# The down-projection's columns as seven block products, its steps spread over the next part's up-projection

## The chip, the core and the metric

The kernel runs on one core of one Trainium2 chip. The metric is device microseconds of one execution of the program. A profile is taken of one execution; its span runs from the first to the last instruction that the profile shows, and the execution's own time is a little longer. All lengths below are in microseconds (us) unless marked ns.

## What is computed

One layer of a streaming encoder, on 256 tokens of width 2048 in fp32. An attention half (two groups of eight heads with a combined input projection and an output projection) comes first and isn't touched in what it computes. The second half is the feed-forward network (FFN), cut here to what matters:

```python
def conv_ffn(h, w_up, conv_w, conv_b, w_down):
    u = h @ w_up                                  # 256 x 2048 @ 2048 x 11264
    u = causal_depthwise_conv(u, conv_w, width=3) + conv_b
    gate, val = jnp.split(u, 2, axis=-1)          # 256 x 5632 each
    return (jax.nn.silu(gate) * val) @ w_down     # 5632 x 2048

x = x + hybrid_mixer(rms_norm(x), ...)            # attention, output projection
x = x + conv_ffn(rms_norm(x), ...)
```

## The kernel before

Matmuls run in fp32r. To keep fp32 accuracy every operand is split into a rounded part `hi` and a remainder `lo`, and a product is three matmuls: hi x hi, hi x lo and lo x hi. Activations are split once and kept; weights are split as they stream in. `weights` (lines 202 to 215) does that for a tile of 128 x 2048 (1 MiB): a DMA on SyncE's queue into `w_raw` (three buffers), a cast on ScalarE into `w_hi` (line 210, two buffers) and a subtraction on VectorE into `w_lo` (line 211, two buffers). The three instructions are put 200 instructions ahead of their place in the program's order of priority (`AHEAD`). The framework orders each engine's instructions by priority and readiness when the program is built; on the chip every engine runs its own list in order.

The kernel has these stages:

- Up to about 413 us: input projection, both attention groups and the output projection. `token_major` (lines 220 to 240) is the projection with tokens on the partitions: the activation tile is the stationary operand, 512 weight columns are the moving one, and per k tile and token tile it issues three matmuls (lines 235 to 237) into an accumulator of two PSUM banks (`psa`, two of them). `next_rows` (line 535) transposes the normalized x into `hT` for the FFN while the output projection ends; `sums_of_squares` (line 163) reads each quarter of x with the scratch tile `junk`. The attention has its own pools `at`, `tmp` (SBUF) and `pss` (PSUM), which close at line 563; the weight buffers (`wpool`) are one pool for the whole kernel.
- The FFN (lines 563 to 633), in three parts of 16, 16 and 12 column tiles of 128 (`FFN_PARTS`). For each part first all of its up-projection, then its down-projection.
- Up-projection: `up_pair` (line 603) makes two column tiles over all 256 tokens. `feature_major` (lines 242 to 260) loads and splits the weights in two halves of eight k tiles; per k and column tile there is one matmul of 512 moving columns (hi of the weights by hi and lo of the activations, line 250) and one of 256 (lo by hi, line 255). Accumulators rotate over three places, two in `psa` and one in `psf`. `convolved` (lines 582 to 601) empties the accumulator (`summed`, lines 262 to 267: a copy on ScalarE and an addition on VectorE), multiplies by the token factors `R` (line 588) into one of four `up` buffers, and makes the convolution (ScalarE line 592, VectorE line 597, two taps per tile). A gate pair and a value pair give the gated activations, split into `g2` (lines 620 to 624).
- Down-projection: for each part and each 512 of the 2048 output columns, `token_major` over the part's k tiles, and an addition of the two token tiles into x in SBUF (line 630). After the last part the results are written out, 512 columns at a time (line 633).

`step` (line 192) is called after each weight tile's matmuls, and lets generators in `waiting` (attention heads, transposes) issue their next piece between two weight tiles.

Of the kernel before, what the change touches and what calls it, by code (L numbers as in the profile page):

```python
# [24 lines left out]
NFT = DFF // P  # L25
# [11 lines left out]

AHEAD = 200
WINDOW = 2
FFN_PARTS = [(0, 16), (16, 32), (32, 44)]  # L40


@with_exitstack
def hybrid_layer(
# [19 lines left out]
    nc = tc.nc  # L64
    act, dve = nc.scalar, nc.vector
# [7 lines left out]
    wpool = ctx.enter_context(tc.tile_pool(name="wpool", bufs=3))  # L73
# [12 lines left out]
    crow = const.tile([NC2, 4, P], F32, name="crow")  # L86
# [21 lines left out]
    def load_parameters(masks):  # L108
        r0 = KT
        for src, n in (  # L110
            (ffn_norm, KT), (out_norm_fox, NH), (out_norm_sb, NH), (q_norm, 1), (k_norm, 1)
        ):
            nc.sync.dma_start(prow[r0 : r0 + n, :], src[0].rearrange("(n p) -> n p", p=P))
            r0 += n
        nc.sync.dma_start(cs[:, P:], cst[:, P:C_MF])
        nc.sync.dma_start(masks, cst[:, C_MF:])
        nc.sync.dma_start(bf, b_forget.to_broadcast([P, NH]))
        nc.sync.dma_start(crow[:, :3, :], conv_w[0].rearrange("w (n p) -> n w p", p=P))
        nc.sync.dma_start(crow[:, 3, :], conv_b[0].rearrange("(n p) -> n p", p=P))

    def rsqrt(out_, ss, scale, n):
        a = small.tile([P, n], F32, name="rs_a", tag=f"rs_a{n}")
# [55 lines left out]
            dve.tensor_scalar(dg[t], ident, rstd[:, t : t + 1], None, op0=ALU.mult)  # L178
        return rstd, dg

    def in_every_partition(dg, n):
        R = const.tile([P, S], F32, name=f"R{n}")
        pr = psb.tile([P, S], F32, name="pr", tag="t")
        for t in range(NT):
            nc.tensor.matmul(pr[:, t * P : (t + 1) * P], ones, dg[t], start=t == 0, stop=t == NT - 1)
        dve.tensor_copy(R, pr)
        return R


    waiting = deque()  # L190

    def step():
        for g in list(waiting)[:WINDOW]:
            if next(g, g) is g:
                waiting.remove(g)
# [3 lines left out]
            step()  # L199


    def weights(src, a, b):
        raw = wpool.tile([P, 2048], F32, name="w_raw", tag="w_raw")
        hi = wpool.tile([P, 2048], F32R, name="w_hi", tag="w_hi", bufs=2)
        lo = wpool.tile([P, 2048], F32R, name="w_lo", tag="w_lo", bufs=2)
        n = a * b
        r3 = raw[:, :n].rearrange("p (a b) -> p a b", a=a)
        with tc.high_priority(offset=AHEAD):
            nc.sync.dma_start(r3, src)
            act.copy(hi[:, :n], raw[:, :n])  # L210
            dve.tensor_tensor(lo[:, :n], raw[:, :n], f32(hi[:, :n]), op=ALU.subtract)  # L211
        return (
            hi[:, :n].rearrange("p (a b) -> p a b", a=a),
            lo[:, :n].rearrange("p (a b) -> p a b", a=a),
        )

    def rows_of(w, k0, n, c0, cols):
        return w[k0 * P : (k0 + n) * P, c0 : c0 + cols].rearrange("(k p) c -> p k c", p=P)
# [23 lines left out]
    def feature_major(w, c0, pool, tag):  # L242

        acc = pool.tile([P, 2, 512], F32, name="pu", tag=tag)
        for kh in range(2):
            hi, lo = weights(rows_of(w, 8 * kh, 8, c0, 2 * P), 8, 2 * P)
            for i in range(8):
                k = 8 * kh + i
                for j in range(2):
                    nc.tensor.matmul(  # L250
                        acc[:, j, :], hi[:, i, j * P : (j + 1) * P],
                        hT[:, k].rearrange("p a b -> p (a b)"), start=k == 0, stop=False,
                    )
                for j in range(2):
                    nc.tensor.matmul(  # L255
                        acc[:, j, S:], lo[:, i, j * P : (j + 1) * P], hT[:, k, 0, :],
                        start=False, stop=k == KT - 1,
                    )
            step()
        return acc  # L260

    def summed(pool, acc, tag, **kw):

        t2 = pool.tile([P, 2, S], F32, name="t2", tag=tag, **kw)
        act.copy(t2, acc[:, :, S:])
        dve.tensor_tensor(t2, acc[:, :, :S], t2, op=ALU.add)
        return t2

    with ExitStack() as actx:
        at = actx.enter_context(tc.tile_pool(name="at", bufs=1))  # L270
        pss = actx.enter_context(tc.tile_pool(name="pss", bufs=2, space=bass.MemoryType.PSUM))
        tmp = actx.enter_context(tc.tile_pool(name="tmp", bufs=2))
# [77 lines left out]
        rstd1, dg1 = token_factors(ss1, 1)  # L350
# [19 lines left out]
        for j in range(3):  # L370
            acc = project(2 * WF + 344 * j, 344)
# [97 lines left out]


        B0 = 3 * WF + NH
        R1 = in_every_partition(dg1, 1)
        R1q = const.tile([P, S], F32, name="R1q")
        dve.tensor_scalar(R1q, R1, QSCALE, None, op0=ALU.mult)

        def sb_heads(c0, scale, name):
# [87 lines left out]
    ccol = const.tile([P, 4, NC2], F32, name="ccol")  # L564
    R = None

    def convolution_parameters():
# [6 lines left out]
    ff = ctx.enter_context(tc.tile_pool(name="ff", bufs=2))  # L574
    psf = ctx.enter_context(tc.tile_pool(name="psf", bufs=1, space=bass.MemoryType.PSUM))
    nu = 4
    up = [ff.tile([P, 2, 2 + S], F32, name=f"up{i}") for i in range(nu)]
    for u in up:
        dve.memset(u[:, :, 0:2], 0.0)
    n_up = 0  # L580

    def convolved(ps, f0):

        nonlocal n_up
        u = up[n_up % nu]
        n_up += 1
        t2 = summed(ff, ps, "t2")
        dve.tensor_tensor(u[:, :, 2:], t2, R.unsqueeze(1).to_broadcast([P, 2, S]), op=ALU.mult)  # L588
        a = ff.tile([P, 2, S], F32, name="cv", tag="cv", bufs=4)
        for j in range(2):  # L590
            f = f0 + j
            act.activation(  # L592
                a[:, j, :], u[:, j, 2:], AF.Identity,
                scale=ccol[:, 2, f : f + 1], bias=ccol[:, 3, f : f + 1],
            )
            for w in range(2):
                dve.scalar_tensor_tensor(  # L597
                    a[:, j, :], u[:, j, w : w + S], ccol[:, w, f : f + 1], a[:, j, :],
                    op0=ALU.mult, op1=ALU.add,
                )  # L600
        return a

    def up_pair(f0):

        nonlocal R, n_pair
        pool, tag = (psf, "pu") if n_pair % 3 == 2 else (psa, "acc")
        n_pair += 1
        acc = feature_major(wu, f0 * P, pool, tag)
        if R is None:
            R = in_every_partition(dg2, 2)  # L610
            convolution_parameters()
        return convolved(acc, f0)

    gT = {}
    n_pair = 0
    for n_part, (f_lo, f_hi) in enumerate(FFN_PARTS):
        for f in range(f_lo, f_hi, 2):
            gate = up_pair(f)
            val = up_pair(NFT + f)
            act.activation(gate, gate, AF.Silu)  # L620
            dve.tensor_tensor(gate, gate, val, op=ALU.mult)
            g2 = ff.tile([P, 2, 2, S], F32R, name="g2", tag="g2", bufs=12)
            act.copy(g2[:, 0], gate)  # L623
            dve.tensor_tensor(g2[:, 1], gate, f32(g2[:, 0]), op=ALU.subtract)
            for j in range(2):
                gT[f + j] = g2[:, :, j, :]
        for c in range(4):
            acc = token_major(lambda k: gT[f_lo + k], wd, f_lo, f_hi - f_lo, 512 * c, 512)
            xs = x2[:, :, c * 512 : (c + 1) * 512]
            dve.tensor_tensor(xs, acc, xs, op=ALU.add)  # L630
            if n_part == len(FFN_PARTS) - 1:
                for t in range(NT):
                    nc.sync.dma_start(of[t * P : (t + 1) * P, c * 512 : (c + 1) * 512], xs[:, t, :])


def _constants():
# [54 lines left out]
```

## Time and profile before

| | us |
|---|---|
| median of 3 runs (1151.68 to 1153.18) | 1152.29 |
| the profiled execution | 1153.37 |
| its span | 1151.6 |
| TensorE matmuls busy (share of the span) | 1137.1 (99%) |
| VectorE busy | 716.4 (62%) |
| ScalarE busy | 551.9 (48%) |

Lines of the profile name the source line, the engine, the operation and the tiles (`out<-in`). PE is TensorE's matmuls, PEld its weight loads, DVE VectorE, ACT ScalarE, SPq the queue of SyncE that issues the DMAs. Matmul records overlap, since the array is pipelined: what one costs in a row of many is the distance from start to start. In the timeline an "x2" merges neighbours of one kind. A releaser, after "<-", is what the profile shows as the last thing that an instruction waited for.

### The profile page before, as it was taken

How to read it: one execution, taken by the hardware profiler on the slowest of the kernel's cores; microseconds unless marked ns; L12 is line 12 of the kernel's file. 1: busy time of each engine (PE TensorE's matmuls, PEld its weight loads, DVE VectorE, ACT ScalarE, POOL GpSimd, SP SyncE). 2: the span in 40 equal slices, each digit the busy share in tenths (PEclk: the TensorE clock that was granted, in tenths of full speed). 3: DMA queues.
4: the chain of work that ended last, by engine and by line, in shares of the span. 5: the costliest groups of instructions: out<-in, count | busy, mean ns of one | idle time of the engine just before them, and what ended most of it. 6: DMA issues, size and time to landing. Idle time of an engine off the chain costs nothing.

```text
span 1151.6 us, 14371 instructions
## 1 busy us (share of the span) xinstructions
PE 1137.1 (99%) x6002; PEld 976.7 (85%) x6002; DVE 716.4 (62%) x798; ACT 551.9 (48%) x620; POOL 0.2 (0%) x4
## 2 busy tenths in 40 slices
PE   7999999999999999999999999999999999999998
PEld 5998888888888888888888888888888888888886
DVE  4646756646565667677774546767775455767753
ACT  4644454455564555555554334555554334555531
POOL 0000000000000000000000000000000000000000
PEclk9999999999999999999999999999999999999999
DMA  6766555564445545555556655555556655555562
GB/s 227 213 210 204 170 173 161 168 182 148 147 149 170 185 154 193 195 194 185 183 183 198 203 183 186 194 196 192 184 183 188 204 193 183 187 195 193 189 221 74
DMA packets 162540, 211.39 MB, mean 184 GB/s; under 512 B 3737, under 2 KB 117547, under 8 KB 162475
## 3 DMA queue, kind: packets, MB, share of 16 engines
q1 hardware_dynamic: 162474, 210.47, 56.7%
q8 instruction: 47, 0.77, 0.3%
q14 instruction: 19, 0.15, 0.0%
HBM read 208.36 MB, written 2.10 MB: 183 GB/s over the span
## 4 chain that ended last, share of the span: by engine, by line
PE 96%; DVE 1%; ACT 1%; DMA 1%; issue 1%; SPq 0%; ACTq 0%; DVEq 0%
PE pu L250 34%; PE pu L255 17%; PE acc L236 14%; PE acc L237 14%; PE acc L235 14%; ACT w_hi L210 1%; DVE w_lo L211 1%; PE ps_x L152 1%; DMA w_raw<-in_w_in_dram 0%; DMA masks<-in_cst_dram 0%; PE ps_z L492 0%; PE ps_h L284 0%; PE ps_s L425 0%; PE ps_o L452 0%; PE ps_o L518 0%
## 5 line engine op out<-in xcount | busy, mean ns | idle before, releaser
L211 DVE TENSOR_TENSOR w_lo<-w_raw,w_hi 128x2048 fp32r<-128x2048 f32 (+2 forms) x204 | 450.8, 2210 | 360.2 <-ACT w_hi L210 360.2
L210 ACT CAST w_hi<-w_raw 128x2048 fp32r<-128x2048 f32 (+2 forms) x204 | 375.9, 1843 | 512.4 <-issue 260.5
L250 PE MATMUL pu<-hT,w_hi 128*128 128x512 f32 x1664 | 523.5, 396 | 0.0
L255 PEld LDWEIGHTS pu<-hT,w_lo 128*128 128x128 f32 x1664 | 312.4, 188 | 73.9 <-DVE w_lo L211 0.4
L255 PE MATMUL pu<-hT,w_lo 128*128 128x256 f32 x1664 | 327.6, 278 | 0.0
L250 PEld LDWEIGHTS pu<-hT,w_hi 128*128 128x128 f32 x1664 | 253.8, 189 | 0.3
L236 PE MATMUL acc<-w_lo,g 128*128 128x512 f32 x352 | 137.1, 389 | 0.8 <-DVE w_lo L211 0.8
L235 PE MATMUL acc<-w_hi,g 128*128 128x512 f32 x352 | 137.1, 389 | 0.0
L237 PE MATMUL acc<-w_hi,g 128*128 128x512 f32 x352 | 136.9, 389 | 0.0
L235 PE MATMUL acc<-w_hi,hT 128*128 128x512 f32 (+1 forms) x320 | 120.2, 376 | 0.0
L236 PE MATMUL acc<-w_lo,hT 128*128 128x512 f32 (+1 forms) x320 | 119.2, 373 | 0.5 <-DVE w_lo L211 0.3
L237 PE MATMUL acc<-w_hi,hT 128*128 128x512 f32 (+1 forms) x320 | 119.0, 372 | 0.0
L236 PEld LDWEIGHTS acc<-w_lo,g 128*128 128x128 f32 x352 | 66.1, 188 | 14.8 <-DVE w_lo L211 1.3
L235 PEld LDWEIGHTS acc<-w_hi,g 128*128 128x128 f32 x352 | 66.1, 188 | 13.8 <-ACT g L623 0.3
L237 PEld LDWEIGHTS acc<-w_hi,g 128*128 128x128 f32 x352 | 66.1, 188 | 13.8
L597 DVE SCALAR_TENSOR_TENSOR cv<-up,ccol,cv 128x256 f32<-128x256 f32 x176 | 74.2, 480 | 2.2 <-ACT cv L592 2.0
L236 PEld LDWEIGHTS acc<-w_lo,hT 128*128 128x128 f32 x320 | 60.5, 189 | 9.6 <-DVE w_lo L211 1.5
L237 PEld LDWEIGHTS acc<-w_hi,hT 128*128 128x128 f32 x320 | 60.6, 189 | 8.8
L235 PEld LDWEIGHTS acc<-w_hi,hT 128*128 128x128 f32 x320 | 60.6, 189 | 8.1
L592 ACT ACTIVATE cv<-up,ccol 128x256 f32<-128x256 f32 x88 | 48.2, 591 | 8.0 <-DVE up L588 8.0
L235 PE MATMUL acc<-w_hi,oT 128*128 128x512 f32 x96 | 38.1, 397 | 0.0
L237 PE MATMUL acc<-w_hi,oT 128*128 128x512 f32 x96 | 37.5, 390 | 0.0
(146 smaller groups left out, 602.4 us busy)
## 6 DMA issues: line engine op xcount, KB each, us to landing
w_raw<-in_w_up_dram SPq DMA_DIRECT2D x88, 1024.0 KB, 5.1
w_raw<-in_w_down_dram SPq DMA_DIRECT2D x44, 1024.0 KB, 5.1
w_raw<-in_w_in_dram SPq DMA_DIRECT2D x36, 1024.0 KB, 5.3
w_raw<-in_w_out_dram SPq DMA_DIRECT2D x16, 1024.0 KB, 5.1
w_raw<-in_w_in_dram SPq DMA_DIRECT2D x12, 688.0 KB, 4.3
w_raw<-in_w_in_dram SPq DMA_DIRECT2D x8, 512.0 KB, 5.3
out_dram<-x SPq DMA_DIRECT2D x8, 256.0 KB, 3.6
x<-in_x_dram SPq DMA_DIRECT2D x3, 512.0 KB, 6.2
```

The lines of the kernel that those rows point to most:

```text
L152: nc.tensor.transpose(ps[:, j, t * P : (t + 1) * P], xt[t][:, (k + j) * P : (k + j + 1) * P], ident)
L210: act.copy(hi[:, :n], raw[:, :n])
L211: dve.tensor_tensor(lo[:, :n], raw[:, :n], f32(hi[:, :n]), op=ALU.subtract)
L235: nc.tensor.matmul(o, lhi, hi[:, i, :], start=first, stop=False)
L236: nc.tensor.matmul(o, lhi, lo[:, i, :], start=False, stop=False)
L237: nc.tensor.matmul(o, llo, hi[:, i, :], start=False, stop=last)
L250: nc.tensor.matmul(acc[:, j, :], hi[:, i, j * P : (j + 1) * P], hT[:, k].rearrange("p a b -> p (a b)"), start=k == 0, stop=False,)
L255: nc.tensor.matmul(acc[:, j, S:], lo[:, i, j * P : (j + 1) * P], hT[:, k, 0, :], start=False, stop=k == KT - 1,)
L592: act.activation(a[:, j, :], u[:, j, 2:], AF.Identity, scale=ccol[:, 2, f : f + 1], bias=ccol[:, 3, f : f + 1],)
L597: dve.scalar_tensor_tensor(a[:, j, :], u[:, j, w : w + S], ccol[:, w, f : f + 1], a[:, j, :], op0=ALU.mult, op1=ALU.add,)
```

## The change

The FFN is cut into six parts, five of eight column tiles and one of four. A part's down-projection is no longer done after its up-projection: it is made a generator, put into `behind`, and issued in steps between the weight tiles of the next part's up-projection. Each weight tile of the up-projection adds `pace` (14, in the last part 22) to a counter, and each 16 of it issue one step, so 14 steps lie among a part's 16 weight tiles, and 11 among the last part's 8. The last part's own down-projection follows at the end as before.

For the first four parts all of the columns, and for the fifth half of them, are computed in blocks: the part's eight k tiles are two row blocks of the weights, 1024 output columns are two column blocks of 512, and the two token tiles are the activation's two. These 2 x 2 x 2 block products are made as seven, on sums and differences of blocks. `combinations` makes four differences or sums of activation blocks for each two pairs, on VectorE, and splits them. `down_in_seven` loads weight blocks, adds them on VectorE, splits each of the seven, multiplies it (12 matmuls, `product`), and adds the bank into x (`add`); two banks go on accumulating over several products. The first weight sum has a buffer of its own, `w_sum`. Two weight blocks are loaded twice, so six loads stand in the place of four.

Around it: the weight buffers are one pool in the attention, closed with it, and a new pool `wff` in the FFN with four `w_raw`, three `w_hi` and three `w_lo`; the convolution's parameters `crow` are loaded at the start of the FFN; the third up-projection accumulator gives its banks to the products; `up` has two buffers for four, `cv` becomes three `gate` and one `val`; `summed` is put 400 instructions ahead.

```diff
-FFN_PARTS = [(0, 16), (16, 32), (32, 44)]
+FFN_PARTS = [(f, min(f + 8, NFT)) for f in range(0, NFT, 8)]
...
+    def load(src, into=None):
+        raw = into if into is not None else wpool.tile([P, 2048], F32, name="w_raw", tag="w_raw")
...
+    def split(raw, a, b):
+        hi = wpool.tile([P, 2048], F32R, name="w_hi", tag="w_hi", bufs=n_split)
+        lo = wpool.tile([P, 2048], F32R, name="w_lo", tag="w_lo", bufs=n_split)
+        act.copy(hi[:, :n], raw[:, :n])
+        dve.tensor_tensor(lo[:, :n], raw[:, :n], f32(hi[:, :n]), op=ALU.subtract)
...
     with ExitStack() as actx:
+        n_split = 2
+        wpool = actx.enter_context(tc.tile_pool(name="wpool", bufs=3))
...
+    n_split = 3
+    wpool = ctx.enter_context(tc.tile_pool(name="wff", bufs=4))
+    psf = ctx.enter_context(tc.tile_pool(name="psf", bufs=2, space=bass.MemoryType.PSUM))
...
+        a11, a21 = g1[:, :, :P], g1[:, :, P:]
+        a12, a22 = g2[:, :, :P], g2[:, :, P:]
+        dve.tensor_tensor(t5, a21, a22, op=ALU.subtract)
+        dve.tensor_tensor(s2, t5, a11, op=ALU.subtract)
+        dve.tensor_tensor(s4, a12, s2, op=ALU.add)
+        dve.tensor_tensor(t7, a11, a21, op=ALU.subtract)
...
+        def product(bank, first, lhs, parts):
+            hi, lo = parts
+            for i in range(4):
+                a, j = divmod(i, 2)
+                for n, (l, r) in enumerate(((0, hi), (0, lo), (1, hi))):
+                    nc.tensor.matmul(bank, lhs(a, l, j), r[:, i, :], ...)
+        def add(to, bank, op=ALU.add):
+            with tc.high_priority(offset=2 * AHEAD):
+                dve.tensor_tensor(to, to, bank, op=op)
...
+        bank_b = psb.tile([P, 512], F32, name="bank_b", tag="t")
+        with ahead():
+            dve.tensor_tensor(w, w, load(w12), op=ALU.add)
+            parts = split(w, 4, 512)
+        product(bank_b, True, of_sums(0), parts)
+        add(x22, bank_b)
+        yield
+        with ahead():
+            b22 = load(w22)
+            parts = split(b22, 4, 512)
+            dve.tensor_tensor(w, w, b22, op=ALU.add)
+        product(bank_b, False, of_sums(2), parts)
+        add(x12, bank_b)
+        yield
...
+        pace = (11 if last_part else 14) * 8 // (f_hi - f_lo)
...
+        if not last_part:
+            behind.append(down_in_seven(f_lo, pairs, sums, 0))
+            if f_hi + 8 > NFT:
+                behind.append(down_plain(f_lo, pairs, 1024, 1024))
+            else:
+                behind.append(down_in_seven(f_lo, pairs, sums, 1024))
```

More of the change, by code (lines that the diff above doesn't have):

```diff
@@ L215, in weights @@
         )
+    def weights(src, a, b):
+        with tc.high_priority(offset=AHEAD):
+            return split(load(src), a, b)
     def rows_of(w, k0, n, c0, cols):
@@ L471, in hybrid_layer @@
         B0 = 3 * WF + NH
[L472 to L473 removed]
+        R1 = in_every_partition(dg1, 1, at)
+        R1q = at.tile([P, S], F32, name="R1q")
         dve.tensor_scalar(R1q, R1, QSCALE, None, op0=ALU.mult)
@@ L571, in convolution_parameters, with convolved @@
             dve.tensor_copy(ccol[:, i, :], pc[:, :NC2])
[L574 to L582, printed above, removed]
+    def convolved(ps, f0, tag, bufs):
         nonlocal n_up
-        u = up[n_up % nu]
+        u = up[n_up % 2]
         n_up += 1
@@ L601, in convolved, with step @@
         return a
[L603 to L608, printed above, removed]
+    behind = deque()
+    n_behind, pace = 0, 0
+    def step():
+        nonlocal n_behind
+        for g in list(waiting):
+            if next(g, g) is g:
+                waiting.remove(g)
+        n_behind += pace
+        while behind and n_behind >= 16:
+            if next(behind[0], behind) is behind:
+                behind.popleft()
+            else:
+                n_behind -= 16
@@ L623, in hybrid_layer @@
             act.copy(g2[:, 0], gate)
             dve.tensor_tensor(g2[:, 1], gate, f32(g2[:, 0]), op=ALU.subtract)
[L625 to L633, printed above, removed]
+            pairs.append(g2)
```

145 lines of the change are left out of this document (120 added, 25 removed).

## The prediction

> **What bounds the kernel now.** I read the page from the top: busy shares, the chain that ended last, then the stages.
>
> ```profile
> span 1151.6 us, 14371 instructions
> PE 1137.1 (99%) x6002; PEld 976.7 (85%) x6002; DVE 716.4 (62%) x798; ACT 551.9 (48%) x620; POOL 0.2 (0%) x4
> ...
> PE 96%; DVE 1%; ACT 1%; DMA 1%; issue 1%; SPq 0%; ACTq 0%; DVEq 0%
> ```
>
> The chain is TensorE for 96% of the span. From about 413 us on, the FFN, it hardly stops. The windows view cuts out one stretch of up-projection and one of down-projection; after the stretch and its length stand busy us (and counts) of PE, PEld, DVE, ACT and POOL, then clock, DMA share and GB/s.
>
> ```profile
> 421.00:599.00 178.00, 178.00 (x1018) 154.79 (x1017) 129.09 (x147) 92.14 (x97) 0.00 (x0) 1.00 0.57 185
> 599.00:690.00 91.00, 91.00 (x416) 75.80 (x415) 46.90 (x27) 33.93 (x20) 0.00 (x0) 1.00 0.60 196
> ```
>
> VectorE is busy 72% of an up-projection stretch and 52% of a down-projection stretch. That slack is what the change spends. Recorded matmuls overlap, so their price is the distance between starts. In the timeline of a down-projection the first and last of 20 consecutive matmuls are
>
> ```profile
> 619.61 0.39 PE L237 MATMUL acc<-w_hi,g 128*128 128x512 f32 x1
> ...
> 623.92 0.39 PE L235 MATMUL acc<-w_hi,g 128*128 128x512 f32 x1
> ```
>
> so one takes (623.92 - 619.61)/19 = 0.227 us. The same view for VectorE, one row of the output projection and then steady up-projection (start, duration, instruction; in brackets the idle time before it):
>
> ```profile
> 403.31 2.29 DVE L211 TENSOR_TENSOR w_lo<-w_raw,w_hi 128x2048 fp32r<-128x2048 f32 x1 [0.58 <-ACT w_hi L210]
> ...
> 439.19 2.29 DVE L211 TENSOR_TENSOR w_lo<-w_raw,w_hi 128x2048 fp32r<-128x2048 f32 x1 [1.70 <-ACT w_hi L210]
> 441.40 0.69 DVE L266 TENSOR_TENSOR t<-pu,t 128x512 f32<-128x512 f32 x1
> 442.12 0.69 DVE L588 TENSOR_TENSOR up<-t,R 128x512 f32<-128x512 f32 x1
> 444.77 2.29 DVE L211 TENSOR_TENSOR w_lo<-w_raw,w_hi 128x2048 fp32r<-128x2048 f32 x1 [1.95 <-ACT w_hi L210]
> 446.98 1.66 DVE L597 SCALAR_TENSOR_TENSOR cv<-up,ccol,cv 128x256 f32<-128x256 f32 x4
> ...
> 450.34 2.29 DVE L211 TENSOR_TENSOR w_lo<-w_raw,w_hi 128x2048 fp32r<-128x2048 f32 x1 [0.97 <-ACT w_hi L210]
> 452.55 0.69 DVE L624 TENSOR_TENSOR g<-cv,g 128x512 fp32r<-128x512 f32 x1
> 453.15 0.69 DVE L266 TENSOR_TENSOR t<-pu,t 128x512 f32<-128x512 f32 x1
> ...
> 455.91 2.29 DVE L211 TENSOR_TENSOR w_lo<-w_raw,w_hi 128x2048 fp32r<-128x2048 f32 x1 [1.35 <-ACT w_hi L210]
> 458.12 1.67 DVE L597 SCALAR_TENSOR_TENSOR cv<-up,ccol,cv 128x256 f32<-128x256 f32 x4
> 461.49 2.29 DVE L211 TENSOR_TENSOR w_lo<-w_raw,w_hi 128x2048 fp32r<-128x2048 f32 x1 [1.70 <-ACT w_hi L210]
> ```
>
> Two things are read here. Two up_pair calls take 461.49 - 439.19 = 22.3 us, so one is 11.15 us of TensorE and half of it, one weight load's worth, 5.57 us. And a subtraction over 2048 elements keeps VectorE for 441.40 - 439.19 = 2.21 us, one over 512 for 0.60 us (452.55 to 453.15) to 0.72 us (441.40 to 442.12, where the next one needs its result).
>
> **The matmuls removed.** A part of eight column tiles and half of the output columns cost 2 row blocks x 2 column blocks x 8 k x 3 = 96 matmuls. As seven products it is 7 x 4 x 3 = 84. Nine such blocks are changed (two in each of the first four parts, one in the fifth): 9 x 12 x 0.227 = **-24.5 us** on an engine that is the chain.
>
> **VectorE's side.** Each block now has seven splits in place of four, four sums of weight tiles, and seven additions into x, each of 512 elements out of PSUM. The activations' combinations are eight subtractions or additions of 256 elements and four of 512 per part. The nearest row to the small ones, and the two sides of a split:
>
> ```profile
> L328 DVE TENSOR_TENSOR ssq<-ssq,osq 128x256 f32<-128x256 f32 x14 | 5.9, 423 | 2.7 <-ACT osq L327 2.7
> ...
> L211 DVE TENSOR_TENSOR w_lo<-w_raw,w_hi 128x2048 fp32r<-128x2048 f32 x184 | 421.8, 2293 | 334.7 <-ACT w_hi L210 334.7
> L210 ACT CAST w_hi<-w_raw 128x2048 fp32r<-128x2048 f32 x184 | 351.5, 1910 | 490.2 <-issue 257.7 <-PE acc L237 190.4 <-PE pu L250 42.1
> ```
>
> While one part's up-projection runs with the previous part's down-projection in it (four such parts, the second to the fifth):
> - TensorE: 8 x 11.15 + 14 x 12 x 0.227 = 89.2 + 38.1 = 127.3 us.
> - VectorE: up-projection 129.09/178 x 89.2 = 64.7; 14 splits and 8 sums x 2.21 = 48.6; 14 additions x 0.66 (the middle of 0.60 and 0.72) = 9.2; combinations 8 x 0.42 + 4 x 0.60 = 5.8. Together 128.3 us.
> - ScalarE: 92.14/178 x 89.2 = 46.2, plus 14 casts x 1.91 and four of the combinations x 0.6 = 75.3 us.
>
> So **VectorE goes from 72% to just over 100% of TensorE's time** in those four parts, without a single wait of its own. In the last part, of four column tiles, TensorE has 4 x 11.15 + 84 x 0.227 + 96 x 0.227 = 85.5 us and VectorE 32.4 + 15 x 2.21 + 11 x 0.66 = 72.8; there TensorE stays the bound, as in the first part, which has no down-projection beside it.
>
> What VectorE loses on top is not in this trace, where it is never full. The lower end is nothing: a full VectorE runs behind, so the casts and matmuls that it waits for are long done. The upper end is the shortest wait among the quoted splits, 0.58 us at 403.31, at each of the 30 splits of a part. I take 0.1 us per split, 3 us per part, near the lower end, because three instead of two buffers for w_hi and w_lo let the cast run one tile ahead. Against it counts what is prepared when the second part begins: two split tiles ahead of TensorE, 5.57 + 2.72 = 8.3 us of matmuls, spent once. The term is 4 x (128.3 + 3 - 127.3) - 8.3 = **+7.7 us** (lower end 0, as 4 x 1.0 is less than 8.3; upper end 4 x (1.0 + 17.4) - 8.3 = +65).
>
> The Trainium skill, "Perfetto Trace Analysis", section "Identifying the Most-Contended Engine" and the strategy after it, says that the same gap repeating on an engine can mean too few buffers for the next tile to be allocated. The rows agree: w_lo waits 1.70, 1.95, 0.97 and 1.35 us for a cast, and 190.4 us of the casts' idle time ended with a matmul that freed a buffer. By that rule alone the third buffer takes the gaps away whole, this term would be 0 and the time 1139, inside the bracket that the forecast is given below.
>
> **The seam ahead of the FFN.** The weight buffers used to be one pool for the whole kernel; now the attention's close with its pools and the FFN opens new ones over the same memory. Does a load into the new pool wait for single old tiles or for all of the attention? The nearest thing in the trace is `up`, already in such a pool. VectorE's and ScalarE's timelines:
>
> ```profile
> 408.75 2.29 DVE L211 TENSOR_TENSOR w_lo<-w_raw,w_hi 128x2048 fp32r<-128x2048 f32 x1 [3.15 <-ACT w_hi L210]
> ...
> 413.12 1.41 DVE L556 SCALAR_TENSOR_TENSOR x<-acc,rg,x 128x512 f32<-128x512 f32 x2 [0.26 <-PE acc L237]
> ...
> 417.42 0.07 DVE L579 MEMSET up<- 128x4 f32 x2
> ```
>
> ```profile
> 415.60 0.61 ACT L167 ACTIVATE junk<-x 128x512 f32<-128x512 f32 x1
> 416.12 0.19 ACT L167 ACTIVATION_READ_ACCUMULATOR junk<-x 128x1 f32 x1
> ```
>
> The memset needs nothing but its memory, VectorE idled 3.15 us ahead of 408.75, and yet it comes only after the attention's last scratch tile `junk` is done at 416.3. I read that as a wait for the whole. Then the first FFN load goes out when the squares of x's last quarter end: x at 413.12 + 1.41 = 414.5, the second square 0.61 + 0.19 later, 415.3. In the old kernel the first up-projection matmul begins here, with its weights long split:
>
> ```profile
> 412.69 0.39 PE L237 MATMUL acc<-w_hi,hT 128*128 128x512 f32 x1
> 412.92 0.62 PE L250 MATMUL pu<-hT,w_hi 128*128 128x512 f32 x2
> ...
> w_raw<-in_w_up_dram SPq DMA_DIRECT2D x88, 1024.0 KB, 5.1
> ```
>
> Now: load 5.1 to 420.4, cast 1.91, w_lo 2.29, so 424.6. TensorE loses 424.6 - 412.9 = 11.7 less about 1.3 that it can do meanwhile (the last transposes, two w_hi matmuls): 10.4 us. It also restarts cold, as at the start of the kernel:
>
> ```profile
> 10.22 0.80 PE L236 MATMUL acc<-w_lo,hT 128*128 128x512 f32 x1
> 10.81 0.63 PE L237 MATMUL acc<-w_hi,hT 128*128 128x512 f32 x1
> 11.23 0.63 PE L235 MATMUL acc<-w_hi,hT 128*128 128x512 f32 x1
> ...
> 14.49 0.48 PE L235 MATMUL acc<-w_hi,hT 128*128 128x512 f32 x1
> 14.81 0.39 PE L236 MATMUL acc<-w_lo,hT 128*128 128x512 f32 x1
> 15.04 0.39 PE L237 MATMUL acc<-w_hi,hT 128*128 128x512 f32 x1
> ```
>
> Starts were 0.42 us apart (10.81 to 11.23) until 14.49, and 0.23 from 14.81 on: about half of the 4.3 us from 10.22 was lost, say 2.0. Together **+12.4 us**; lower end 0, if single tiles are waited for. The Trainium skill, "TensorE: Matmul & The Clock Gate", section "What's actually happening", halves the clock after an idle window of about 3.4 us and for about 3.4 us of work; as an estimate from that page the cold part would be 1.7 us in place of 2.0.
>
> **The rest.** The last down-projection's one stall of matmuls goes, since two plain steps of 24 matmuls, 10.9 us, now stand between the last up-projection and its gate: **-0.9 us**.
>
> ```profile
> 1094.92 0.50 PE L236 MATMUL acc<-w_lo,g 128*128 128x512 f32 x1 [0.85 <-DVE w_lo L211]
> ```
>
> Costed at nothing: the added loads, two more per block. A part has 28 of 1 MiB in 127.3 us, 231 GB/s, against 185 now, and near the kernel's start the queue moved more:
>
> ```profile
> 5.00:14.00 9.00, 5.87 (x17) 4.15 (x16) 4.12 (x6) 3.68 (x6) 0.00 (x0) 1.00 0.93 316
> ```
>
> All loads stand in SP's one queue, and a load that waits for its buffer holds those behind it; four raw buffers at 4.5 us a load leave 18 us for a landing of 5.1 and a split, so this cover is large. Four of a block's seven products add onto a bank that VectorE must have read first; 5.57 us of up-projection lies between, against 0.7 for the addition. If VectorE lags by two splits (4.4 us) that cover is gone, which belongs to the slow rival. The third accumulator is gone too: two remain, each with 11.15 us and more to be emptied. The parameters' load moved to the FFN lies beside 11 us of matmuls.
>
> **The sum** against the profiled execution, 1153.4 us (span 1151.6 plus 1.8): -24.5 + 7.7 + 12.4 - 0.9 = -5.3, so 1148.1. That execution lies 1.1 us above the median of 1152.3; the forecast beside the median is **1147 us**.
>
> **Rivals.** The view of waits (who waited for whom: us in total, times, longest) has one long row for VectorE:
>
> ```profile
> DVE w_lo L211 <- ACT w_hi L210: 360.2, 201, 4.1
> ```
>
> - *No seam.* Loads wait for single tiles, so the new buffers fill while the output projection ends. For: the old weight buffers lie where the new ones will, and the last split there starts at 403.31 and is over 2.3 us later. Against: the late memset. Without the 12.4, 1147 - 12.4 = 1135; without any VectorE loss 1127.
> - *VectorE takes over, slower than before.* It serves one queue in order; a sum, its cast and its w_lo are a chain through ScalarE, and behind a w_lo that waits stand the additions that free PSUM and the split for the next half. For: 360.2 us of such waits now, and no slack at all to hide them. Against: a third buffer, and ScalarE at 59%. At 0.3 us per split the term is 4 x (1.0 + 9) - 8.3 = 31.7 instead of 7.7: 1171 us. At 0.58 it is 65: 1204. It decides from a loss of 0.15 us per split: 4 x (1.0 + 4.5) - 8.3 = 13.7 eats the remaining gain.
> - *Nothing left.* The losses just cancel the 24.5: seam 12.4 and 0.13 to 0.17 us per split, 1150 to 1154.
>
> **How the numbers follow.** Forecast (1138 to 1150) 0.36; no seam (1127 to 1138) 0.20; nothing left 0.12; VectorE takes over 0.32. A measurement of this kernel tells about 0.2%, 2.3 us, from no change. Faster 0.56, same 0.12, slower 0.32. The range cuts off the best of the second case and the worse half of the last: 1130 to 1177.
>
> **What would show it.** TensorE's matmul groups of the down-projection should be 108 fewer. VectorE's busy share should be 95% or more between the second part and the fifth, with idle PE there released by w_lo. Between the output projection and the first up-projection TensorE should idle about 7 to 11 us, with the first w_up load issued after the last `junk`. If VectorE is under 90% there and PE still idles, the order in the queues is the cause and my term of 3 us per part is wrong; if the seam shows no idle time, the reading of the memset is.

## The result: 3.5% slower, and where the 41 us lie

The changed kernel takes 1193.05 us (median of 4 runs, 1192.37 to 1194.88) against 1152.41 (1151.68 to 1153.18), a ratio of 1.0355 with a 95% interval of 1.0337 to 1.0373. The forecast was 1147 and the range ended at 1177. The profiled execution took 1194.88 us. The page of the changed kernel, the lines that answer to those shown of before:

```profile
span 1193.1 us, 14521 instructions
...
PE 1144.6 (96%) x5894; PEld 970.8 (81%) x5894; DVE 904.9 (76%) x978; ACT 616.8 (52%) x667; POOL 0.2 (0%) x4
...
PE   7999999999999899997999899998999979998998
...
DVE  4646656565565666788899989998899989999864
...
PEclk9999999999999989998999989998999989998999
...
PE 90%; DVE 4%; ACT 3%; DMA 2%; issue 1%; SPq 0%; ACTq 0%; DVEq 0%
```

Of 6002 matmuls 5894 are left, 108 fewer, as predicted. TensorE is still the chain, but only for 90% of it. In the clock's row (PEclk, the clock that TensorE was granted) an 8 stands six times: once where the FFN begins and once at each of five places that I call borders, early in a part's up-projection, where the first products of the part before stand. The second part's up-projection begins at 514.0, and TensorE stops at 540.7. The windows view of the first border, of the stretch from there to the next one, of the two together and of the same stretch one part later (busy us and counts of PE, PEld, DVE, ACT, POOL, then clock, DMA share and GB/s):

```profile
540.70:552.00 11.30, 5.33 (x13) 3.58 (x14) 10.31 (x11) 5.86 (x6) 0.00 (x0) 0.63 0.65 221
552.00:678.80 126.80, 126.78 (x668) 107.78 (x667) 116.05 (x112) 70.22 (x61) 0.00 (x0) 0.99 0.66 213
540.70:678.80 138.10, 132.12 (x680) 111.37 (x680) 126.35 (x122) 76.07 (x67) 0.00 (x0) 0.96 0.66 214
678.80:817.70 138.90, 132.93 (x680) 111.97 (x680) 125.97 (x120) 75.99 (x67) 0.00 (x0) 0.96 0.65 212
```

**The loss isn't spread over a part; it stands at its border.** Between borders TensorE is busy for 126.78 of 126.80 us, beside a VectorE that is busy for 116.05, or 92%. In the 11.3 us of the border TensorE works 5.33 us, at 0.63 of its clock, while VectorE has hardly a gap. A part takes 138.1 or 138.9 us where 127.3 were worked out.

To place the difference I took the distances from each FFN matmul's start to the next in both traces and sorted what exceeds the kernel before's distance for the same kind: excess of over 0.06 us is idle time, unless the distance is about doubled (cold clock); less than that is spacing. Where idle time ends and cold clock begins is uncertain by a microsecond or two, their sum isn't. From the 128th up-projection matmul on, and with the seam measured up to it:

| term, us | predicted | measured |
|---|---|---|
| 108 matmuls fewer | -24.5 | -24.5 |
| VectorE's loss, 0.1 us per split | +7.7 | about 0 between borders |
| idle time, nearly all at the five borders | 0 | +37.5 (38.7 against 1.2 before; the predicted -0.9 is in it) |
| cold clock after it | 0 | +12.4 |
| seam ahead of the FFN | +12.4 | +9.9 |
| down-projection matmuls 0.233 us apart, not 0.227 | 0 | +6.2 |
| sum | -5.3 | +41.5, as the spans: 1193.1 - 1151.6 |

**What TensorE waits for at a border.** The waits view of the changed kernel (us in total, times, longest):

```profile
PE bank_b L675 <- ACT s L650: 10.3, 5, 2.3
PE bank_a L675 <- ACT w_hi L208: 9.8, 5, 2.0
...
PE bank_b L675 <- DVE s L651: 6.9, 5, 1.7
```

Each comes five times, once per border. `s` holds the split combinations of the part's activations. The timeline of TensorE at the first border (start, duration; in brackets the idle time before):

```profile
540.30 0.39 PE L257 MATMUL pu<-hT,w_lo 128*128 128x256 f32 x2
543.02 0.50 PE L675 MATMUL bank_b<-w_hi,s 128*128 128x512 f32 x1 [2.32 <-ACT s L650]
...
545.43 1.22 PE L675 MATMUL bank_b<-w_hi,s 128*128 128x512 f32 x2 [1.66 <-DVE s L651]
546.45 0.63 PE L675 MATMUL bank_b<-w_lo,s 128*128 128x512 f32 x1
546.88 0.63 PE L675 MATMUL bank_b<-w_hi,s 128*128 128x512 f32 x1
549.49 0.79 PE L675 MATMUL bank_a<-w_hi,s 128*128 128x512 f32 x1 [1.99 <-ACT w_hi L208]
```

From 546.45 the starts are 0.43 us apart: the clock has halved. On VectorE, the way to that `s` from the addition that empties the part's last value accumulator:

```profile
518.15 0.68 DVE L269 TENSOR_TENSOR t<-pu,t 128x512 f32<-128x512 f32 x1
...
519.94 2.29 DVE L698 TENSOR_TENSOR w_sum<-w_sum,w_raw 128x2048 f32<-128x2048 f32 x1
522.14 2.29 DVE L209 TENSOR_TENSOR w_lo<-w_raw,w_hi 128x2048 fp32r<-128x2048 f32 x1
...
524.74 0.68 DVE L597 TENSOR_TENSOR up<-t,R 128x512 f32<-128x512 f32 x1
527.32 2.29 DVE L209 TENSOR_TENSOR w_lo<-w_sum,w_hi 128x2048 fp32r<-128x2048 f32 x1 [1.89 <-ACT w_hi L208]
...
532.37 2.29 DVE L706 TENSOR_TENSOR w_sum<-w_sum,w_raw 128x2048 f32<-128x2048 f32 x1
534.57 0.88 DVE L606 SCALAR_TENSOR_TENSOR val<-up,ccol,val 128x256 f32<-128x256 f32 x2
535.51 2.29 DVE L209 TENSOR_TENSOR w_lo<-w_raw,w_hi 128x2048 fp32r<-128x2048 f32 x1
...
538.64 0.69 DVE L766 TENSOR_TENSOR gate<-gate,val 128x512 f32<-128x512 f32 x1
...
542.48 2.29 DVE L209 TENSOR_TENSOR w_lo<-w_raw,w_hi 128x2048 fp32r<-128x2048 f32 x1 [0.96 <-ACT w_hi L208]
544.69 1.29 DVE L651 TENSOR_TENSOR s<-t,s 128x512 fp32r<-128x512 f32 x2
```

The small instructions of the chain (L269, L597, L606, L766, L645 to L647, L651) are well under 10 us of work. They take 28, from 518.15 to 544.69 + 1.29, because splits and weight sums, the new down-projection's first ones and the up-projection's own, are put 200 instructions ahead in the same list and go first. The second product's first six matmuls use the earlier combination and ran at 533.56; its other six need the last pairs' `s`, and TensorE, in order, can't pass them to the up-projection behind them. So at the border TensorE waits for VectorE, then ScalarE for TensorE (the cast into the next `w_hi` needs a buffer that those matmuls hold), then TensorE for that cast (1.99 us), and so on.

**The seam.** From the timeline of all engines:

```profile
412.73 0.39 PE L239 MATMUL acc<-w_hi,hT 128*128 128x512 f32 x1
413.15 5.03 SPq L201 DMA_DIRECT2D w_raw<-in_w_up_dram  x4
...
415.20 0.18 ACT L163 ACTIVATION_READ_ACCUMULATOR junk<-x 128x1 f32 x1
...
415.53 0.07 DVE L582 MEMSET up<- 128x4 f32 x2
...
418.16 1.90 ACT L208 CAST w_hi<-w_raw 128x2048 fp32r<-128x2048 f32 x1 [1.00 <-DMA w_raw<-in_w_up_dram]
...
420.11 1.22 PE L252 MATMUL pu<-hT,w_hi 128*128 128x512 f32 x2 [0.40 <-ACT w_hi L208]
```

The loads go out at 413.15, when the output projection's last matmul ends, and not after `junk`, 2 us later. All four go at once, though the old pool's last split had left its `w_raw` at 405.6. The up-projection starts 420.11 - 412.92 = 7.2 us later than before, and its 128th matmul comes at 447.03 in place of 437.12, so 2.7 us of cold clock are in the 9.9.

### The profile page after: what moved, and what is told of

Read it like the earlier page. It is cut to its first block, busy times and chain, and to the rows that moved or that the text cites. A ratio compares the mean times of both kernels' runs of the same rounds, so it can differ in the third digit from the quotient of the medians.

```text
span 1193.1 us, 14521 instructions
## 1 busy us (share of the span) xinstructions
PE 1144.6 (96%) x5894; PEld 970.8 (81%) x5894; DVE 904.9 (76%) x978; ACT 616.8 (52%) x667; POOL 0.2 (0%) x4
## 4 chain that ended last, share of the span: by engine, by line
PE 90%; DVE 4%; ACT 3%; DMA 2%; issue 1%; SPq 0%; ACTq 0%; DVEq 0%
PE pu L252 31%; PE pu L257 15%; PE bank_a L675 8%; PE acc L238 8%; PE acc L237 8%; PE acc L239 8%; PE bank_b L675 5%; ACT w_hi L208 2%; DVE w_lo L209 2%; PE bank_c L675 2%; PE bank_a L747 1%; PE bank_a L749 1%; PE bank_a L748 1%; PE ps_x L148 1%; DMA x<-in_x_dram 0%
## 5 line engine op out<-in xcount | busy, mean ns | idle before, releaser
L208 ACT CAST w_hi<-w_sum 128x2048 fp32r<-128x2048 f32 x36 | 68.7, 1909 | 68.7 <-PE pu L252 46.5
L209 DVE TENSOR_TENSOR w_lo<-w_sum,w_hi 128x2048 fp32r<-128x2048 f32 x36 | 82.3, 2287 | 14.0 <-ACT w_hi L208 14.0
L675 PE MATMUL bank_b<-w_hi,s 128*128 128x512 f32 x144 | 58.7, 466 | 17.2 <-ACT s L650 10.3
L675 PE MATMUL bank_a<-w_hi,s 128*128 128x512 f32 x144 | 51.6, 418 | 9.8 <-ACT w_hi L208 9.8
L675 PEld LDWEIGHTS bank_b<-w_hi,s 128*128 128x128 f32 x144 | 31.9, 226 | 27.9 <-ACT s L650 11.8
L675 PE MATMUL bank_a<-w_hi,g 128*128 128x512 f32 x144 | 48.1, 395 | 0.0
L675 PEld LDWEIGHTS bank_a<-w_hi,s 128*128 128x128 f32 x144 | 28.4, 197 | 18.7 <-ACT w_hi L208 12.8
L606 DVE SCALAR_TENSOR_TENSOR gate<-up,ccol,gate 128x256 f32<-128x256 f32 x88 | 38.6, 481 | 3.6 <-ACT gate L601 3.4
L606 DVE SCALAR_TENSOR_TENSOR val<-up,ccol,val 128x256 f32<-128x256 f32 x88 | 38.2, 480 | 0.9 <-ACT val L601 0.7
L237 PE MATMUL acc<-w_hi,oT 128*128 128x512 f32 x96 | 38.1, 397 | 0.0
```

The source lines that it names most:

```text
L237: nc.tensor.matmul(o, lhi, hi[:, i, :], start=first, stop=False)
L606: dve.scalar_tensor_tensor(a[:, j, :], u[:, j, w : w + S], ccol[:, w, f : f + 1], a[:, j, :], op0=ALU.mult, op1=ALU.add,)
L675: nc.tensor.matmul(bank, lhs(a, l, j), r[:, i, :], start=first and i + n == 0, stop=i == 3 and n == 2, skip_group_check=not first,)
```

## The experiments

Two theories first. A: the borders are a matter of order, the last pairs' convolution and sums behind the new part's splits, and the rest of VectorE's load fits. B: VectorE is too full, and any order loses about the same.

**The sums of the first combination for both.** Every product does the same work, but none waits for the last pairs' sums. It leaves the second combination out of the products, so its output isn't the layer's.

```diff
-            return lambda a, part, j: sums[a][:, part, q, j, :]
+            return lambda a, part, j: sums[0][:, part, q, j, :]
```

> Every product that needs sums of activations takes those of the part's first combination for both halves of its rows; the second combination is still computed by VectorE and ScalarE, but no product reads it (so the output is not the reference's). All work stays, only the wait for the late sums at the part's border goes. Theory A (each of the five borders costs about 10 us because TensorE, in order, stands behind a product whose sums come at the end of a long chain in VectorE's queue, and then runs cold): 1193 - 5 x 10 = 1143 us, with no idle TensorE at 540 us and the like and clock 1.0 there. Theory B (VectorE is simply full, whatever it does, as in the prediction's slow rival): 1188 to 1195.

Measured 1180.61 us (1178.61 to 1181.72), ratio 1.024 (1.0225 to 1.0255): between the two. The wait for `s` is gone, and at the same border another one stands, two products later. TensorE, then VectorE of this kernel:

```profile
542.43 0.40 PE L675 MATMUL bank_a<-w_hi,s 128*128 128x512 f32 x1
547.54 0.80 PE L675 MATMUL bank_a<-w_lo,s 128*128 128x512 f32 x1 [4.71 <-DVE w_lo L209]
```

```profile
540.87 2.28 DVE L717 TENSOR_TENSOR w_raw<-w_raw 128x2048 f32<-128x2048 f32 x1
543.07 0.68 DVE L682 TENSOR_TENSOR x<-x,bank_b 128x512 f32<-128x512 f32 x1
543.67 0.68 DVE L769 TENSOR_TENSOR g<-gate,g 128x512 fp32r<-128x512 f32 x1
...
544.61 0.68 DVE L651 TENSOR_TENSOR s<-t,s 128x512 fp32r<-128x512 f32 x1
545.21 2.28 DVE L209 TENSOR_TENSOR w_lo<-w_sum,w_hi 128x2048 fp32r<-128x2048 f32 x1
```

The needed w_lo of 545.21 stands behind a weight sum of the next product (L717), an addition into x and the rest of the part's end. So it isn't one dependence: both the part's end and the products' beginning fall into the same 30 us of VectorE's list, and whichever goes second is late.

**Plain products alone.** No combinations, no block sums, four splits in place of seven; the spreading and the pools stay.

```diff
-        pace = (11 if last_part else 14) * 8 // (f_hi - f_lo)
+        pace = 8 * 8 // (f_hi - f_lo)
...
-            behind.append(down_in_seven(f_lo, pairs, sums, 0))
...
+            behind.append(down_plain(f_lo, pairs, 0, 2048))
```

> The same six parts, pools, buffers and spreading, but all columns as plain products (96 matmuls a block), with no sums of weights or activations. Both theories: no border waits, VectorE at about 75%; it prices what the spreading and the new pools cost by themselves. Seam 9 us and a matmul spacing of 0.233 in place of 0.227 us on 1056 matmuls (7 us): 1152 + 16 = 1168. If the seam and the spacing cost nothing, 1152.

Measured 1169.32 us (1168.72 to 1170.79), ratio 1.0146 (1.0131 to 1.0161), as expected. Without the added VectorE work TensorE doesn't stop at the border that lies in this stretch:

```profile
540.00:678.00 138.00, 138.00 (x724) 117.07 (x723) 91.67 (x89) 64.14 (x58) 0.00 (x0) 1.00 0.58 191
```

The seam (about 8 us) and the spacing (7.0) are its whole loss, and have nothing to do with the seven products.

**The chain first.** The convolution, the gate, `g2` and the combinations are put 400 instructions ahead, as `summed` is (five blocks put under `with tc.high_priority(offset=2 * AHEAD)`).

> Convolution, gate, g2 and the combinations are put 400 instructions ahead, like the accumulator's emptying, so that VectorE's list takes them before the splits. Work unchanged. Theory A: the chain from the last accumulator to the sums falls from 27 us to 10 to 15, most of the border wait goes: 1145 to 1165. Theory B: unchanged, 1188 to 1195, or worse, as the splits come later.

Measured 1174.51 us (1172.83 to 1176.72), ratio 1.0184 (1.0167 to 1.0201): again between. Now the splits are late instead: TensorE idles 26 us, waiting for `w_hi` and `w_lo` of both projections. Turning the order of the two bursts round moves the wait and leaves two thirds of it.

**Later steps.** The products' steps begin two weight tiles later (three in the last part) and then come faster, so the part's end and their beginning no longer meet: in the second part's up-projection the first product stood 11.1 us after the start and now stands at 22.3, the second at 30.7 for 19.5. The expectation below has three tiles and 14 us for this, which is too much.

```diff
-        n_behind = 0
...
-        pace = (11 if last_part else 14) * 8 // (f_hi - f_lo)
+        pace = 36 if last_part else 18
+        n_behind = -3 * pace
```

> The steps of a part's down-projection start three weight tiles later (at the fourth of 16) and run one per tile from there; in the last part two per tile. The product that needs the late sums comes about 14 us later. Theory A: the border waits go, 1143 to 1155. Theory B: the same work is pressed into 13 of 16 tiles, so it is no faster, 1190 to 1200.

Measured 1164.94 us (1162.23 to 1166.22), ratio 1.0103 (1.0086 to 1.012). This is 28 us less than the change with the same work in it, and nearer A, though not within its bounds: idle time falls from 38.7 to 18.4 us and the cold part from 12.4 to 3.3. **The borders are a matter of order.** What stayed is read from its waits:

```profile
ACT t L268 <- DVE s L651: 11.0, 7, 2.1
...
PE pu L252 <- DVE t L269: 8.1, 4, 2.0
```

Once per part an accumulator is emptied too late, since ScalarE's copy of it waits for a `t2` that the combinations still use.

**Own buffers for the combinations.** On top of the later steps; the room comes from one `w_raw`.

```diff
-    wpool = ctx.enter_context(tc.tile_pool(name="wff", bufs=4))
+    wpool = ctx.enter_context(tc.tile_pool(name="wff", bufs=3))
...
-        t = [ff.tile([P, 2, 2, P], F32, name="t2", tag="t2") for _ in range(2)]
+        t = [ff.tile([P, 2, 2, P], F32, name="t5", tag="t5") for _ in range(2)]
```

> The version with later steps, with two buffers of their own for the combinations' t in place of the two t2 that they share with summed, and three w_raw buffers in place of four, which makes the room. Theory A (the 2.0 us that TensorE still idles once in a part before L252 come from the shared t2: ScalarE cannot copy the next accumulator into a t2 before the combinations have left it): four of these stalls go, 1165 - 8 = 1157 us, 1154 to 1160. Theory B (VectorE's list as such is what is late there; another operation is then the last one, and the stall only moves): 1163 to 1167. The three w_raw are taken to cost nothing, since no wait for the loads shows between the borders.

Measured 1159.4 us (1154.72 to 1161.33), ratio 1.0049 (1.003 to 1.0068): A. Both waits are gone from the list, and VectorE is now busy for 125 of 130 us in the second and third part, with TensorE at 128.6 to 128.8:

```profile
560.00:690.00 130.00, 128.63 (x678) 108.53 (x677) 124.75 (x121) 75.51 (x66) 0.00 (x0) 1.00 0.68 227
```

So VectorE at 96% of its time leaves TensorE at 99%, and theory B, that VectorE is too full in any order, is out.

**The seam by itself: a kept weight pool.** On the version with plain products; one `wpool` (three `w_raw`, two `w_hi`, two `w_lo`) from the start, as before the change.

```diff
+    n_split = 2
+    wpool = ctx.enter_context(tc.tile_pool(name="wpool", bufs=3))
     big = ctx.enter_context(tc.tile_pool(name="big", bufs=1))
...
-        n_split = 2
-        wpool = actx.enter_context(tc.tile_pool(name="wpool", bufs=3))
...
-    n_split = 3
-    wpool = ctx.enter_context(tc.tile_pool(name="wff", bufs=4))
```

> The version with plain products alone (1169 us, no waits at the borders), with one weight pool opened at the start and kept, three w_raw and two w_hi and w_lo as before the change, so that the up-projection's first loads need not wait for attention's memory. Theory A (the seam comes from the closed pool): the 128th matmul of the up-projection comes 8 to 10 us sooner and the time is 1159 to 1162. Theory B (something else holds the up-projection's start, the norm's sums or the order in the queues): within 2 us of 1169. Apart from that, if the down-projection's matmuls go back to 0.2267 us apart only because the weights stand at other addresses, another 7 us are gone, 1152 to 1155.

Measured 1162.33 us (1162.01 to 1162.44), ratio 1.008 (1.0066 to 1.0093), 7.0 less than with the new pool and 0.3 above theory A's range. The up-projection's 128th matmul is at 436.6, as before the change (437.1) and 8.6 us sooner than with the new pool. The seam is the closed pool. The matmuls stay 0.2333 us apart.

**The spacing by itself: two gaps.** Also on the version with plain products. An unused tile ahead of `gate` and `g2` shifts where these two and `t2` begin; the weight buffers stay in place.

```diff
+    ff.tile([P, 16], F32, name="gap", bufs=1)
```

> The version with plain products alone (1169 us), with an unused tile of 64 bytes in a partition ahead of gate and g2 and nothing else changed. The stationary operand of the down-projection's matmuls then begins at an address that is 96 over a multiple of 128 bytes, as before the change, and not 32 over. Theory A (the 0.2333 us between these matmuls, against 0.2267 before, hang on where the stationary operand begins): 0.2267 again, 960 x 0.0067 = 6.4 us less, 1162 to 1164. Theory B (they hang on the moving operand's place, or on what the other engines do beside them): 0.2333 and 1168 to 1170.

Measured 1168.93 us (1168.12 to 1169.37), ratio 1.0135 (1.012 to 1.0151): 0.2322 us in place of 0.2333, and theory A as I had put it fell. The second gap is the same line with 48 in place of 16.

> The version with plain products alone (1169 us), with an unused tile of 192 bytes in a partition ahead of gate and g2, so that the down-projection's stationary operand begins a multiple of 256 bytes from where its moving operand begins, as in the kernel before (64 bytes over in the version with plain products, 128 with the gap of 64). Theory A (the distance of 0.2333 us hangs on this offset): 0.2267 us again and 1162 to 1164. Theory B (it hangs on something else): 0.232 to 0.234 and 1168 to 1170.

Measured 1163.27 us (1162.19 to 1164.52), ratio 1.0098 (1.0083 to 1.0113): A. The first and last of 20 consecutive matmuls of the last down-projection, of the changed kernel and of this one:

```profile
1179.65 0.40 PE L237 MATMUL acc<-w_hi,g 128*128 128x512 f32 x1
...
1184.08 0.39 PE L238 MATMUL acc<-w_lo,g 128*128 128x512 f32 x1
```

```profile
1148.21 0.39 PE L237 MATMUL acc<-w_hi,g 128*128 128x512 f32 x1
...
1152.51 0.39 PE L238 MATMUL acc<-w_lo,g 128*128 128x512 f32 x1
```

4.43/19 = 0.233 us and 4.30/19 = 0.226.

**Everything mended, first try.** Later steps, own buffers, the kept pool with two split buffers each, the gap of 64.

> Later steps, own buffers for t, the kept weight pool (three w_raw, two w_hi and w_lo, w_sum beside them) and the 64 bytes ahead of g2, all with the seven products in place. Theory A (seam, borders, shared buffer and spacing are separate costs, and what is left is the 108 matmuls fewer): 1165 - 8 - 10 - 6 = 1141 us, 1136 to 1147, below the kernel before. Theory B (with VectorE at nine tenths, two w_hi and w_lo in place of three bring the waits back): 1152 to 1170.

Measured 1246.81 us (1243.15 to 1252.36), ratio 1.0817 (1.0793 to 1.0842): B, and far beyond the price that I had put on it. Four things differ here, so the suspect was tried alone, on the version with later steps and own buffers:

```diff
-    n_split = 3
+    n_split = 2
```

> Later steps and own buffers for t, three w_raw (1159 us), with two w_hi and two w_lo in place of three and nothing else changed. Theory A (the third pair of split buffers is what lets the splits run ahead of TensorE while VectorE is at nine tenths; its loss is the whole of what the kernel with everything mended lost): seam as with three, so about 1247 + 8 = 1255, 1240 to 1265. Theory B (that loss came from the kept pool itself or from w_sum's new place): 1158 to 1165.

Measured 1261.01 us (1257.47 to 1263.8), ratio 1.0941 (1.0919 to 1.0963): A. With two `w_hi` and `w_lo` TensorE stops for about a microsecond at weight tile after weight tile, and VectorE, for want of a free buffer, is busy for only 115 of 140 us. Its waits and one stretch:

```profile
PEld pu L257 <- DVE w_lo L209: 72.9, 51, 3.2
PE pu L257 <- DVE w_lo L209: 51.5, 50, 2.7
```

```profile
560.00:700.00 140.00, 123.95 (x616) 101.32 (x616) 114.72 (x110) 66.83 (x59) 0.00 (x0) 0.96 0.59 195
```

**Everything mended, with three.** The kept pool of three `w_raw` and two `w_hi` and `w_lo`, and a third pair that the FFN opens and every third split takes.

```diff
-        hi = wpool.tile([P, 2048], F32R, name="w_hi", tag="w_hi", bufs=n_split)
...
+        n_splits += 1
+        third = ff is not None and n_splits % 3 == 0
+        pool, bufs = (ff, 1) if third else (wpool, 2)
+        hi = pool.tile([P, 2048], F32R, name="w_hi", tag="w_hi", bufs=bufs)
```

> Later steps, own buffers for t, the weight pool kept from the start (three w_raw, two w_hi and w_lo) and a third w_hi and w_lo that the feed-forward part opens and every third split takes, no gap. Theory A (seam and borders are separate costs): 1159 - 8 = 1151 us, 1148 to 1154, about the time before. Theory B (the kept pool brings waits of its own): 1156 or more.

Measured 1145.52 us (1145.11 to 1146.3), ratio 0.9942 (0.9928 to 0.9955): below the kernel before, and 2.5 us below the lower end of what I expected. Part of that is the spacing: every third product, on the third pair, runs at 0.2268 us. And with the gap of 192:

> The same with the gap of 192 bytes ahead of gate and g2. Theory A (the offset of the stationary operand sets 0.2333 or 0.2267 us): another 6 us less, 1145, 1142 to 1149, below the kernel before. Theory B (the offset is nothing): within 2 us of the same kernel without the gap.

Measured 1142.99 us (1140.26 to 1144.34), ratio 0.9918 (0.9906 to 0.993), the fastest of all, though the gap is worth 2.5 us and not 6. The spacing did come down to 0.228 (its excess from 5.0 us to 1.0), but idle time rose from 11.1 to 14.6. That VectorE is late more often beside a faster TensorE fits this, but isn't shown: it is one profile of each kernel, and this one is of the slowest of five executions (1144.34). Its page and a part:

```profile
DVE  4646756646565677789999999999999999999964
...
PEclk9999999999999999999999999999999999999999
```

```profile
560.00:690.00 130.00, 129.09 (x687) 110.34 (x686) 126.46 (x122) 76.75 (x68) 0.00 (x0) 1.00 0.69 229
```

In this part VectorE is at 97%, and TensorE still at 99%.

## Why the prediction was wrong, point by point

- **The matmuls removed:** right, 108 fewer and -24.5 us.
- **VectorE's side, the demand:** right. 128.3 us per part were worked out, 126.35 and 125.97 measured.
- **VectorE's side, the loss: the step that failed.** I priced it as a little per split, spread evenly, and took as the lower end that a full VectorE only runs behind, so that what it waits for is long done. That speaks of VectorE's own waits and not of what TensorE waits for. Of the waits that the products add I named only the banks that VectorE must have read, and priced them at nothing. The wait of the second product for the combinations of the part's last pairs was in the diff and in no term, and the question what stands between those pairs and their `s` in VectorE's list wasn't asked. With the waits that follow it at the same border it cost about 50 us, idle and cold, where the term was +7.7; without it alone (the first experiment) the late `w_lo` took its place and only 12 us came back. No price per split describes it: between borders it was nothing, at a border about 10 us. The rival "VectorE takes over" had the engine and the sign, but not the place; that its two times, 1171 and 1204, lie on either side of the measured one is luck. Later steps alone, at the same number of splits, gave back 28 us.
- **The signs** that I had set didn't tell the cases apart. VectorE was to be at 95% or more, or under 90% if the order in the queues was the cause. It is at 91% (126.35 of 138.10 us, 125.97 of 138.90), between the two, and the order was the cause; TensorE's idle time was to be released by `w_lo`, and at the first four borders the first release is `s`.
- **The price of 0.1 us per split** comes out where the order is mended, but only as an average: the fastest version has 14.6 - 1.2 us of idle time and 2.2 of cold clock, 15.6 together, over the 139 splits that lie beside or behind the other work (4 x 30 and 19), 0.11 each. It isn't spread over them. Some 10 us stand in four places, once a part, where the second block's first products begin (from 586.9, 715.7, 846.2 and 977.8), and some 6 in the last part. So that 0.1 fits is in part luck. With two buffers in place of three, each split costs (1255.7 - 1157.3)/139 = 0.7 us more. That I took the third buffer as a reason for a low price was right, and so was the rule that the prediction quoted: the Trainium skill, "Perfetto Trace Analysis", section "Optimization Strategy", lets a gap that repeats on an engine mean too few buffers. Here a gap of about a microsecond came 50 times with two buffers and went with the third. The time that this rule alone gave, 1139 us, failed for the same reason as the forecast: it has no word on the borders.
- **The seam:** right in kind, 9.9 us for 12.4. The load waited for the old weight pool's last reader, at 413.1, and not for all of the attention: the memset, my evidence, stands in VectorE's list behind the sum that needs `junk` and says nothing of its own memory. TensorE idles for only 4.5 of the 7.2 us by which the up-projection starts later (0.84, 0.22, 3.02 and 0.40); the rest are transposes and the four matmuls that make `R`.
- **The cold clock** was counted at the seam and nowhere else, and there as 2.0 us where 2.7 were measured. At a border no single idle stretch is longer than 2.32 us (2.32, 1.66, 1.99, with six recorded matmuls between them), and still the clock halved. By the windows view it was 1.00 from 540.7 to 543.5 and 0.50 from 543.7 to 545.4, so it halved after the first stretch of 2.32 us and two matmuls. The Trainium skill, "TensorE: Matmul & The Clock Gate", section "HAM oscillation — how this bites in real kernels", warns of idle gaps of more than about 3.4 us; the rows of the border show the halving after a shorter one, so the measurement decides.
- **The price of a matmul**, 0.227 us, was taken from before for all of the new ones; they took 0.233, 6.2 us in all.
- **The added loads:** as predicted, no wait for a DMA stands at a border, and 1145 us were reached with the same loads. With three `w_raw` ScalarE's casts wait 15.1 us in all for up-projection loads (fastest version); what TensorE loses by that wasn't measured.

## What to carry to other kernels

When work is spread over another stage, don't only add up each engine's demand: at every place where the pieces change over, write down which instruction needs the newest result, and read off the in-order list what was put ahead of its producers. In this kernel VectorE at 96 to 97% cost little while the splits could run a buffer ahead, and two buffers in place of three cost about 100 us; count buffers before counting busy time. Keep long-lived streaming buffers in a pool that outlives the stage, since a new pool over the old one's memory cost a whole load, cast and clock ramp here.

## What the hardware showed beyond that

The distance between matmuls of 512 moving columns depended on where the two operands begin in a partition. By the built programs' addresses the stationary operand `g2` began a multiple of 256 bytes from the moving `w_hi` and `w_lo` in the kernel before and with the gap of 192 (0.2267 us), 64 bytes over in the change and with plain products (0.2333) and 128 over with the gap of 64 (0.2322). In the mended version without a gap, the products on the third pair of split buffers, which lies a multiple of 256 from `g2`, took 0.2268 and those on the other two 0.2333 and 0.2327, in one and the same run. Offsets other than these three, and the up-projection's form, weren't tried.
